# A two-layer expert trunk on one core: gate matrix by one matmul per token, v rows by fours

## Chip, core and metric

One core of one Trainium2 chip. The metric is the device time of one execution in microseconds (us); three runs of the kernel before gave 3102.27 to 3110.34, median 3108.2.

## What is computed

Two layers over 512 tokens of width 1024, in float32. Layer 0 mixes tokens by sliding-window attention, layer 1 by a gated convolution of width 3. After each mixer comes an expert layer that takes most of the work:

```python
def peer_ffn(xn, w_query, sub_keys, expert_u, expert_v):
    q = (xt @ w_query).reshape(T, PEER_HEADS, 2, QUERY_HALF)
    s = jnp.einsum('thpd,hpnd->thpn', q, sub_keys)
    s_top, i_top = lax.top_k(s, PEER_TOPK)
    ...
```

Each of 8 heads chooses 16 of 16384 experts per token, so a token has 128 experts, with a gate for each. Expert e is a row of u and a row of v: the output of a token is the sum over its experts of gate x gelu(x . u[e]) x v[e].

## The kernel before

Tokens are four tiles of 128. The expert layer is done in two ways at once.

Tiles 0 and 1 go the way of `gather` (line 625). For every one of 128 choices an indirect DMA, issued by POOL, fetches the u rows of 128 tokens into a gather tile (line 636), and DVE dots them with x into a column of `act` (line 639). Then for each token an indirect DMA fetches its 128 v rows (line 667), and PE multiplies them by a one-hot column of weights `wd` into 32 rows of `acc` (line 677), four matmuls for a pair of tokens; a manual dependency makes the first of them wait for both rows. Gather tiles come from `gtile` (line 617): GAT = 6 of them, and at times a few more from a pool that another stage leaves free.

Tiles 2 and 3 go the way of `dense` (line 693): all 16384 experts in 128 blocks per layer. `ustep` loads a block of u (`du`), ACT rounds it (`uh`, line 701), DVE takes the rest (`ul`, line 702), PE makes 24 matmuls of 256 columns into `psA` (lines 180 to 183), ACT applies gelu into `dw` (line 712). `vstep` multiplies `dw` by a row of the gate matrix G (line 718; on DVE, or on POOL while a u gather runs), splits it (`wh`, `wl`) and v (`vh`, `vl`), and PE makes 12 matmuls into `y` (line 736).

G holds for each block, token and expert the gate, mostly zero. It is made in chunks of IC = 32 blocks, four chunks per layer, by `gen` (line 739) for TG = 16 tokens at a time. DVE builds a one-hot of the expert's low index (`oj`, line 745), one of its high index (`oi`, line 748), and two products of that with the high and low halves of the gate (line 751). PE multiplies `oj` by each half into the same 32 columns of a PSUM bank, `psG`, one token after the other (line 756), so a group has 32 matmuls. ACT scales the bank into four G buffers of 8 blocks (line 759). `psG` has one bank. G has GB = 5 such buffers of 8 blocks, one of which holds the first gelu results of the layer (`pre`).

The first chunk of a layer is made ahead of its first `vstep`; the next chunks during the last 8 steps (`q0` = 24) of the chunk before. Here "tail" is the end of such a stretch, before the first step that needs the new chunk.

The order of work: `dense`, `gather` and the routing and mixing of the layers are generators that `merge` (line 816) interleaves, by the pace that each yields (`GY` after a group in the first chunk, `rate()` in the gathers). Tile's scheduler then sets the order on every engine from a timeline of its own, with priorities raised by HPG for `gens` and HPV or HPF for the v matmuls. Each engine takes its instructions strictly in that order.

Of the kernel before, what the change touches and what calls it, by code (L numbers as in the profile page):

```python
# [8 lines left out]
F32 = mybir.dt.float32  # L9
# [25 lines left out]
TG = 16  # L35
IC = 32
HC = 8
GAT = 6
# [8 lines left out]
GB = 5  # L47
# [3 lines left out]
GY = 1.7  # L51
# [4 lines left out]
PRE = 1  # L56
# [28 lines left out]
def trunk(ctx: ExitStack, tc: tile.TileContext, a: dict, out: bass.AP):  # L85
# [539 lines left out]
    def gather(l, t, r):  # L625
# [28 lines left out]
        for gr in range(2):  # L654
            acc = pv.tile([P, 512], F32, name="acc", tag="acc")
            for q in range(4):
                wd = gp.tile([P, 2, 8, 32], F32, name="wd", tag="wd", bufs=2)
                wdf = wd.rearrange("p j r c -> p j (r c)")
                nc.gpsimd.memset(wd, 0.0)
                nc.vector.tensor_copy(wdf[:, :, 8 * q:8 * q + 7 * 33 + 1:33],  # L660
                                      wT.rearrange("p (j r) -> p j r", j=4)[:, 2 * gr:2 * gr + 2, 8 * q:8 * q + 8])
                for r8 in range(8):
                    vgs = []
                    for j in range(2):
                        tt = 64 * gr + 32 * j + 8 * q + r8
                        vg = gtile("vg")
                        ld = nc.gpsimd.indirect_dma_start(  # L667
                            out=vg, out_offset=None, in_=a[f"v{l}"],
                            in_offset=bass.IndirectOffsetOnAxis(ap=idxT[:, tt:tt + 1], axis=0))
                        vgs.append(vg)  # L670
                        if j == 0:
                            yield rate()
                    with tc.high_priority(offset=HPF if st.get("front") else HPV):
                        for j in range(2):
                            for h in range(2):
                                c = 32 * (2 * j + h)
                                mm = nc.tensor.matmul(acc[c:c + 32, :], wd[:, j, r8, :],  # L677
                                                      vgs[j][:, h * 512:(h + 1) * 512],
                                                      start=(q == 0 and r8 == 0), stop=(q == 3 and r8 == 7))
                                if j == 0:  # L680
                                    tc.add_manual_dep(mm.ins, ld.ins.name, together, reason="both rows of a pair")
                    yield rate()
# [10 lines left out]
    def dense(l, rs, pool):  # L693
# [11 lines left out]
        def ustep(i):  # L705
# [4 lines left out]
            w = (pre[:, i, :] if i < npre else  # L710
# [4 lines left out]
        def vstep(i):  # L715
            first, last = i == 0, i == NK - 1
            w = ws.pop(i)
            (nc.gpsimd if (WPU if st.get("gu") else WPV) else nc.vector).tensor_tensor(w, w, G[i // HC][:, i % HC, :], op=ALU.mult)
            f = VU if st.get("gu") else VG if i % IC >= 2 * IC - GB * HC else VB0
# [19 lines left out]
        def gen(i, tg):  # L739
# [13 lines left out]
            ps = pmm("psG")  # L753
            for T in range(TG):
                for q in range(2):
                    nc.tensor.matmul(ps[:, T * IC:(T + 1) * IC], oj[:, :, T], oi[:, q, :, T],  # L756
                                     start=(q == 0), stop=(q == 1))
            for hf in range(IC // HC):
                nc.scalar.mul(G[i // HC + hf][:, :, tg * TG:(tg + 1) * TG],  # L759
                              ps.rearrange("p (t i) -> p i t", i=IC)[:, hf * HC:(hf + 1) * HC, :], 1.0 / GSC)  # L760

        NG = T2 // TG
        G = {}

        def gens(c, tg):
            if tg == 0:
                for hf in range(IC // HC):
                    G[c * (IC // HC) + hf] = pool.tile([P, HC, T2], F32, name="G", tag="G", bufs=GB)
            with tc.high_priority(offset=HPG):
                gen(c * IC, tg)  # L770

        npre = HC * PRE
        pre = pool.tile([P, HC, T2], F32, name="pre", tag="G", bufs=GB) if PRE else None
# [6 lines left out]
        for i in range(NK):  # L780
            c, q = divmod(i, IC)
            q0 = 2 * IC - GB * HC
# [211 lines left out]
```

## Time and profile before

| | before |
|---|---|
| median of three runs | 3108.2 us (3102.27 to 3110.34) |
| the profiled execution's own time | 3084.04 us |
| its span in the profile | 3082.2 us |
| PE busy, mean granted clock | 2782.4 us (90%), 0.95 |
| DVE busy | 2255.1 us (73%) |
| ACT, POOL busy | 1178.1 (38%), 1352.1 (44%) |
| DMA | 931.40 MB, mean 302 GB/s |

Busy time of PE is that of its matmuls; weight loads (PEld) stand apart and overlap them. In a row of a group, "idle before" is idle time of that engine right before the group's instructions, and the arrow names what ended it. The granted clock of PE is a share of its full 2.4 GHz, 0.50 being its lower level of 1.2 GHz. Dense steps are numbered 0 to 127 in layer 0 and 128 to 255 in layer 1; the first `y` of layer 0 is at 665 us, that of layer 1 at 2118.

### The profile page before, as it was taken

The numbers are of one execution on the slowest core, as the hardware profiler recorded it, in microseconds if no ns is written. First come the engines' busy times: TensorE is split into PE (matmuls) and PEld (weight loads), VectorE is DVE, ScalarE is ACT, GpSimd is POOL, SyncE is SP. The second block draws the span as 40 slices with busy tenths as digits, with TensorE's granted clock in tenths as the row PEclk, the third lists the DMA queues.
The fourth block names the chain that finished last, engine by engine and source line by source line (L and its number), as shares of the span: only waits on it lengthen the run. The fifth ranks groups of instructions, "written<-read, shape, count | busy, mean of one in ns | idle before, by whom it ended". The sixth has DMA issues, their size and how long they took to land.

```text
span 3082.2 us, 53493 instructions
## 1 busy us (share of the span) xinstructions
PE 2782.4 (90%) x19980; PEld 2242.6 (73%) x19980; DVE 2255.1 (73%) x5363; ACT 1178.1 (38%) x2414; POOL 1352.1 (44%) x1154
## 2 busy tenths in 40 slices
PE   5964799999998999999997798999998798999998
PEld 5862367757986887778776787775787687778776
DVE  2499859887996997455459998887479999456444
ACT  4225433424333334344343334333434333334433
POOL 0157643354354444531347752345326866531331
PEclk8986899979999999999999899997999999999999
DMA  5888888879889977985999996787959988975996
GB/s 193 299 312 307 323 303 292 307 278 359 299 329 381 356 268 260 328 301 178 350 335 387 373 359 220 264 306 270 319 193 377 357 297 321 340 274 182 341 338 215
DMA packets 263205, 931.40 MB, mean 302 GB/s; under 512 B 29984, under 2 KB 38560, under 8 KB 262944
## 3 DMA queue, kind: packets, MB, share of 16 engines
q0 software_dynamic: 147456, 536.94, 48.1%
q1 hardware_dynamic: 115488, 391.03, 35.2%
q8 instruction: 158, 2.59, 0.3%
q14 instruction: 103, 0.84, 0.1%
HBM read 916.31 MB, written 11.53 MB: 301 GB/s over the span
## 4 chain that ended last, share of the span: by engine, by line
PE 72%; DVE 14%; DMA 5%; issue 4%; ACT 3%; POOL 1%; SPq 0%; DVEq 0%; ACTq 0%; POOLq 0%
PE y L736 20%; PE acc L677 9%; PE psG L756 9%; PE psA L180 8%; PE psA L181 7%; PE psA L183 7%; DVE ug L639 7%; PE psrq L568 3%; DMA ug<-in_u_dram,idx 2%; PE psbcu L404 1%; DMA vg<-in_v_dram,idxT 1%; PE psq L241 1%; DVE vl L702 1%; PE psrs L574 1%; PE psrq L180 1%
## 5 line engine op out<-in xcount | busy, mean ns | idle before, releaser
L667 POOL DMA_INDIRECT vg<-in_v_dram,idxT x512 | 550.0, 1074 | 945.7 <-PE acc L677 839.0
L636 POOL DMA_INDIRECT ug<-in_u_dram,idx x512 | 670.3, 1309 | 626.5 <-DVE act L639 269.8
L639 DVE CUSTOM_DVE_ANT_0 ug<-ug,xn 128x1024 f32<-128x1024 f32 x512 | 628.8, 1240 | 27.5 <-DMA ug<-in_u_dram,idx 26.7
L180 PE MATMUL psA<-xh,uh 128*128 128x256 f32 x2048 | 525.5, 294 | 44.7 <-ACT uh L701 26.8
L702 DVE TENSOR_TENSOR ul<-du,uh 128x1024 fp32r<-128x1024 f32 x256 | 316.4, 1236 | 264.5 <-ACT uh L701 244.9
L181 PE MATMUL psA<-xl,uh 128*128 128x256 f32 x2048 | 503.7, 284 | 0.0
L180 PEld LDWEIGHTS psA<-xh,uh 128*128 128x128 f32 x2048 | 391.9, 191 | 147.6 <-ACT wh L724 54.5
L702 DVE TENSOR_TENSOR vl<-dv,vh 128x1024 fp32r<-128x1024 f32 x256 | 319.9, 1249 | 183.5 <-ACT vh L701 169.4
L701 ACT CAST uh<-du 128x1024 fp32r<-128x1024 f32 x256 | 269.5, 1053 | 340.7 <-PE psA L181 296.4
L181 PEld LDWEIGHTS psA<-xl,uh 128*128 128x128 f32 x2048 | 391.5, 191 | 5.3 <-issue 3.0
L701 ACT CAST vh<-dv 128x1024 fp32r<-128x1024 f32 x256 | 268.8, 1051 | 240.8 <-PE y L736 198.3
L677 PE MATMUL acc<-vg,wd 128*32 128x512 f32 x2048 | 315.8, 637 | 10.4 <-DMA vg<-in_v_dram,idxT 10.0
L756 PEld LDWEIGHTS <-oj 128*128 128x128 f16 x4096 | 278.1, 159 | 63.1 <-issue 37.6
L736 PE MATMUL y<-vh,wh 128*128 128x512 f32 x1024 | 291.5, 404 | 26.6 <-ACT vh L701 26.6
L756 PE MATMUL psG<-oi,oj 128*128 128x32 f16 x4096 | 298.4, 249 | 7.6 <-ACT G L759 6.6
L183 PE MATMUL psA<-xh,ul 128*128 128x256 f32 x2048 | 292.2, 284 | 5.3 <-DVE ul L702 5.3
L736 PE MATMUL y<-vl,wh 128*128 128x512 f32 x1024 | 281.7, 397 | 11.6 <-DVE vl L702 11.6
L183 PEld LDWEIGHTS psA<-xh,ul 128*128 128x128 f32 x2048 | 264.4, 190 | 23.5 <-issue 9.2
L736 PE MATMUL y<-vh,wl 128*128 128x512 f32 x1024 | 278.7, 394 | 0.0
L759 ACT ACTIVATE G<-psG 128x128 f32<-128x128 f32 x512 | 102.5, 282 | 366.5 <-PE psG L756 346.2
L745 DVE TENSOR_TENSOR oj<-ijT,iorep 128x2048 f16<-128x2048 f16 x128 | 157.8, 1233 | 108.9 <-PE psG L756 108.6
L736 PEld LDWEIGHTS y<-vh,wh 128*128 128x128 f32 x1024 | 181.1, 192 | 71.4 <-ACT vh L701 35.1
(207 smaller groups left out, 3902.6 us busy)
## 6 DMA issues: line engine op xcount, KB each, us to landing
du<-in_uT_dram SPq DMA_DIRECT2D x256, 512.0 KB, 6.2
dv<-in_v_dram SPq DMA_DIRECT2D x256, 512.0 KB, 6.2
wpc<-in_wq_dram SPq DMA_DIRECT2D x64, 512.0 KB, 5.7
wpc<-in_w_in_dram SPq DMA_DIRECT2D x48, 512.0 KB, 6.7
wpo<-in_wo_dram SPq DMA_DIRECT2D x16, 512.0 KB, 4.5
ug<-in_u_dram,idx POOLq DMA_INDIRECT x512, 7.3
vg<-in_v_dram,idxT POOLq DMA_INDIRECT x512, 6.9
wpo<-in_w_out_dram SPq DMA_DIRECT2D x16, 512.0 KB, 7.3
```

Source lines behind the costliest of these rows:

```text
L180: nc.tensor.matmul(ps, w[0][:, k, :], x[0][:, k, ts], start=(k == 0), stop=False)
L181: nc.tensor.matmul(ps, w[0][:, k, :], x[1][:, k, ts], start=False, stop=False)
L183: nc.tensor.matmul(ps, w[1][:, k, :], x[0][:, k, ts], start=False, stop=(k == KC - 1))
L636: nc.gpsimd.indirect_dma_start(out=ug, out_offset=None, in_=a[f"u{l}"], in_offset=bass.IndirectOffsetOnAxis(ap=r["idx"][h][:, c:c + 1], ax ...
L639: nc.vector.tensor_tensor_reduce(out=ug, in0=ug, in1=xn, scale=1.0, scalar=0.0, op0=ALU.mult, op1=ALU.add, accum_out=act[:, s:s + 1])
L667: ld = nc.gpsimd.indirect_dma_start(out=vg, out_offset=None, in_=a[f"v{l}"], in_offset=bass.IndirectOffsetOnAxis(ap=idxT[:, tt:tt + 1], ax ...
L677: mm = nc.tensor.matmul(acc[c:c + 32, :], wd[:, j, r8, :], vgs[j][:, h * 512:(h + 1) * 512], start=(q == 0 and r8 == 0), stop=(q == 3 and ...
L701: nc.scalar.copy(hi, w)
L702: nc.vector.tensor_tensor(lo, w, hi, op=ALU.subtract)
L736: nc.tensor.matmul(ys[tt][h], x[:, tt * P:(tt + 1) * P], m[:, h * 512:(h + 1) * 512], start=first and k == 0, stop=last and k == len(terms ...
L745: nc.vector.tensor_tensor(oj, jT.unsqueeze(1).to_broadcast([P, P, TG]), iorep, op=ALU.is_equal)
L756: nc.tensor.matmul(ps[:, T * IC:(T + 1) * IC], oj[:, :, T], oi[:, q, :, T], start=(q == 0), stop=(q == 1))
```

## The change

Four things are changed. `gen` takes 8 tokens instead of 16, with one-hot tiles of half the size. Each token has one matmul of 64 columns instead of two of 32 that accumulate: the products with the high and the low half of the gate stand in separate columns of the bank, and the addition moves to the evacuation, where ACT writes the first half scaled into G and DVE adds the second with scalar_tensor_tensor. G is one ring of GR = 40 rows instead of five buffers of 8; where a chunk's 32 rows pass the end of the ring the evacuation is in two pieces. And `gather` multiplies four v rows at a time, when all four have come, from GAT = 8 gather tiles. In the new kernel the `psG` matmul is line 758, ACT's piece 767, DVE's addition 768, `oj` 747, `oi` 750 and 753, the u dots 638, `ul` and `vl` 704, `uh` and `vh` 703, gelu 714, the multiplication by G 720, `wl` 727.

```diff
-TG = 16
+TG = 8
 IC = 32
-HC = 8
-GAT = 6
+TP = 8
+GAT = 8
...
-GB = 5
+GR = 40
...
-GY = 1.7
+GY = 0.85
...
-PRE = 1
@@ -659,26 +658,29 @@
                 nc.gpsimd.memset(wd, 0.0)
                 nc.vector.tensor_copy(wdf[:, :, 8 * q:8 * q + 7 * 33 + 1:33],
                                       wT.rearrange("p (j r) -> p j r", j=4)[:, 2 * gr:2 * gr + 2, 8 * q:8 * q + 8])
-                for r8 in range(8):
-                    vgs = []
-                    for j in range(2):
-                        tt = 64 * gr + 32 * j + 8 * q + r8
+                for r8 in range(0, 8, 2):
+                    vgs, lds = [], []
+                    for n in range(4):
+                        tt = 64 * gr + 32 * (n % 2) + 8 * q + r8 + n // 2
                         vg = gtile("vg")
                         ld = nc.gpsimd.indirect_dma_start(
                             out=vg, out_offset=None, in_=a[f"v{l}"],
                             in_offset=bass.IndirectOffsetOnAxis(ap=idxT[:, tt:tt + 1], axis=0))
                         vgs.append(vg)
-                        if j == 0:
+                        lds.append(ld)
+                        if n < 3:
                             yield rate()
                     with tc.high_priority(offset=HPF if st.get("front") else HPV):
-                        for j in range(2):
+                        for n in range(4):
+                            j, r = n % 2, r8 + n // 2
                             for h in range(2):
                                 c = 32 * (2 * j + h)
-                                mm = nc.tensor.matmul(acc[c:c + 32, :], wd[:, j, r8, :],
-                                                      vgs[j][:, h * 512:(h + 1) * 512],
-                                                      start=(q == 0 and r8 == 0), stop=(q == 3 and r8 == 7))
-                                if j == 0:
-                                    tc.add_manual_dep(mm.ins, ld.ins.name, together, reason="both rows of a pair")
+                                mm = nc.tensor.matmul(acc[c:c + 32, :], wd[:, j, r, :],
+                                                      vgs[n][:, h * 512:(h + 1) * 512],
+                                                      start=(q == 0 and r == 0), stop=(q == 3 and r == 7))
+                                if n < 3:
+                                    for ld in lds[n + 1:]:
+                                        tc.add_manual_dep(mm.ins, ld.ins.name, together, reason="rows of four")
                     yield rate()
             for j in range(2):
                 for h in range(2):
@@ -707,7 +709,7 @@
             u = pool.tile([P, KC, P], F32, name="du", tag="raw", bufs=RB)
             nc.sync.dma_start(u, a[f"uT{l}"][i])
             mm3(ps[:, :T2], halves(u, [P, KC, P], "u"), (xh, xl), slice(0, T2))
-            w = (pre[:, i, :] if i < npre else
+            w = (G[:, IC + i, :] if i < npre else
                  pool.tile([P, T2], F32, name="dw", tag="dw", bufs=LAG + 2))
             nc.scalar.activation(w, ps[:, :T2], AF.Gelu)
             ws[i] = w
@@ -715,8 +717,8 @@
         def vstep(i):
             first, last = i == 0, i == NK - 1
             w = ws.pop(i)
-            (nc.gpsimd if (WPU if st.get("gu") else WPV) else nc.vector).tensor_tensor(w, w, G[i // HC][:, i % HC, :], op=ALU.mult)
-            f = VU if st.get("gu") else VG if i % IC >= 2 * IC - GB * HC else VB0
+            (nc.gpsimd if (WPU if st.get("gu") else WPV) else nc.vector).tensor_tensor(w, w, G[:, i % GR, :], op=ALU.mult)
+            f = VU if st.get("gu") else VG if i % IC >= 2 * IC - GR else VB0
             sp = int((i + 1) * f) > int(i * f)
             if sp:
                 wh = pool.tile([P, T2], F32R, name="wh", tag="wh", bufs=2)
@@ -750,27 +752,30 @@
             for q in range(2):
                 nc.vector.tensor_tensor(oi[:, q], oi[:, 2],
                                         rr["gb"][:, q:q + 1, t0:t0 + TG].to_broadcast(sh), op=ALU.mult)
-            ps = pmm("psG")
-            for T in range(TG):
-                for q in range(2):
-                    nc.tensor.matmul(ps[:, T * IC:(T + 1) * IC], oj[:, :, T], oi[:, q, :, T],
-                                     start=(q == 0), stop=(q == 1))
-            for hf in range(IC // HC):
-                nc.scalar.mul(G[i // HC + hf][:, :, tg * TG:(tg + 1) * TG],
-                              ps.rearrange("p (t i) -> p i t", i=IC)[:, hf * HC:(hf + 1) * HC, :], 1.0 / GSC)
+            for part in range(TG // TP):
+                ps = pmm("psG")
+                for T in range(TP):
+                    nc.tensor.matmul(ps[:, T * 2 * IC:(T + 1) * 2 * IC].rearrange("p (q i) -> p q i", q=2),
+                                     oj[:, :, part * TP + T], oi[:, 0:2, :, part * TP + T], start=True, stop=True)
+                psv = ps.rearrange("p (t q i) -> p q i t", q=2, i=IC)
+                tok = slice(tg * TG + part * TP, tg * TG + (part + 1) * TP)
+                r0 = i % GR
+                cut = min(IC, GR - r0)
+                for o, n, row in ((0, cut, r0), (cut, IC - cut, 0)):
+                    if n:
+                        g = G[:, row:row + n, tok]
+                        nc.scalar.mul(g, psv[:, 0, o:o + n, :], 1.0 / GSC)
+                        nc.vector.scalar_tensor_tensor(g, psv[:, 1, o:o + n, :], 1.0 / GSC, g,
+                                                       op0=ALU.mult, op1=ALU.add)
 
         NG = T2 // TG
-        G = {}
+        G = pool.tile([P, GR, T2], F32, name="G")
 
         def gens(c, tg):
-            if tg == 0:
-                for hf in range(IC // HC):
-                    G[c * (IC // HC) + hf] = pool.tile([P, HC, T2], F32, name="G", tag="G", bufs=GB)
             with tc.high_priority(offset=HPG):
                 gen(c * IC, tg)
 
-        npre = HC * PRE
-        pre = pool.tile([P, HC, T2], F32, name="pre", tag="G", bufs=GB) if PRE else None
+        npre = GR - IC
         for i in range(LAG + npre):
             ustep(i)
             yield 1.0
@@ -779,7 +784,7 @@
             yield GY
         for i in range(NK):
             c, q = divmod(i, IC)
-            q0 = 2 * IC - GB * HC
+            q0 = 2 * IC - GR
             if q >= q0 and c + 1 < NK // IC:
                 for tg in range((q - q0) * NG // (IC - q0), (q - q0 + 1) * NG // (IC - q0)):
                     gens(c + 1, tg)
```

Groups of `psG` matmuls go from 128 of 32 to 256 of 8, and their evacuation from 512 pieces on ACT to 448 on ACT and 448 on DVE. In PE's order, groups that follow the group before with no other matmul between go from 5 to 85: 12, 2, 10 and 13 by chunk in layer 0, and 13, 6, 11 and 18 in layer 1. Separate stretches of `acc` matmuls go from 238 to 159. Three places show it.

ACT in the tail of layer 0's last chunk, before (`G` is the evacuation, `uh`, `vh`, `dw`, `wh` belong to dense steps):

```order
L759 ACTIVATE G<-psG 128x8x16 x4
L701 CAST uh<-du 128x1024
L712 ACTIVATE dw<-psA 128x256
L759 ACTIVATE G<-psG 128x8x16 x4
L701 CAST vh<-dv 128x1024
L724 CAST wh<-dw 128x256
```

and now:

```order
L767 ACTIVATE G<-psG 128x24x8
L703 CAST uh<-du 128x1024
L767 ACTIVATE G<-psG 128x8x8
L714 ACTIVATE dw<-psA 128x256
L703 CAST vh<-dv 128x1024
L714 ACTIVATE dw<-psA 128x256
L767 ACTIVATE G<-psG 128x24x8
L767 ACTIVATE G<-psG 128x8x8
L767 ACTIVATE G<-psG 128x24x8
```

Four pieces in a row, with a dense step's work between, have become pieces of 8 and 24 rows that each have something of their own to wait for; the last rows stand one after the other with nothing between.

DVE at the same place, before (`oj`, `oi` the one-hots, `ul`, `vl`, `wl` the splits of dense steps):

```order
L718 TENSOR_TENSOR dw<-dw,G 128x256
L745 TENSOR_TENSOR oj<-ijT,iorep 128x2048
L748 TENSOR_TENSOR oi<-ijT,iorep 128x512
L751 TENSOR_TENSOR oi<-oi,gb 128x512 x2
L702 TENSOR_TENSOR vl<-dv,vh 128x1024
L725 TENSOR_TENSOR wl<-dw,wh 128x256
L745 TENSOR_TENSOR oj<-ijT,iorep 128x2048
```

and now:

```order
L753 TENSOR_TENSOR oi<-oi,gb 128x256 x2
L704 TENSOR_TENSOR ul<-du,uh 128x1024
L768 SCALAR_TENSOR_TENSOR G<-psG,G 128x8x8
L704 TENSOR_TENSOR vl<-dv,vh 128x1024
L747 TENSOR_TENSOR oj<-ijT,iorep 128x1024
L750 TENSOR_TENSOR oi<-ijT,iorep 128x256
L768 SCALAR_TENSOR_TENSOR G<-psG,G 128x24x8
L753 TENSOR_TENSOR oi<-oi,gb 128x256 x2
L768 SCALAR_TENSOR_TENSOR G<-psG,G 128x8x8
L747 TENSOR_TENSOR oj<-ijT,iorep 128x1024
```

One group's one-hots now stand around the two additions of the group before: `oj` and `oi` ahead of the first, the two gated `oi` between them.

DVE beside dense steps and a u gather in layer 1, one step, before (`ug`, `act` are a dot and its sum):

```order
L702 TENSOR_TENSOR vl<-dv,vh 128x1024
L725 TENSOR_TENSOR wl<-dw,wh 128x256
L639 ISA ug,act<-ug,xn 128x1024
L639 ISA act 128x1
L702 TENSOR_TENSOR ul<-du,uh 128x1024
L718 TENSOR_TENSOR dw<-dw,G 128x256
L639 ISA ug,act<-ug,xn 128x1024
L639 ISA act 128x1
L639 ISA ug,act<-ug,xn 128x1024
L639 ISA act 128x1
```

and now:

```order
L704 TENSOR_TENSOR ul<-du,uh 128x1024
L727 TENSOR_TENSOR wl<-dw,wh 128x256
L638 ISA ug,act<-ug,xn 128x1024
L638 ISA act 128x1
L638 ISA ug,act<-ug,xn 128x1024
L638 ISA act 128x1
L720 TENSOR_TENSOR dw<-dw,G 128x256
L638 ISA ug,act<-ug,xn 128x1024
L638 ISA act 128x1
L638 ISA ug,act<-ug,xn 128x1024
L638 ISA act 128x1
L704 TENSOR_TENSOR vl<-dv,vh 128x1024
```

Three u rows stand beside each dense step before, four now. By dense step 56 of layer 0, DVE has dotted 256 u rows before and 312 now; in layer 1 the second u phase ends at step 192 before and 160 now.

## Rows read from the trace of the kernel before

**Rows 1.** The page: span, busy time by engine, the chain that ended last.
```profile
span 3082.2 us, 53493 instructions
...
PE 2782.4 (90%) x19980; PEld 2242.6 (73%) x19980; DVE 2255.1 (73%) x5363; ACT 1178.1 (38%) x2414; POOL 1352.1 (44%) x1154
...
PE 72%; DVE 14%; DMA 5%; issue 4%; ACT 3%; POOL 1%; SPq 0%; DVEq 0%; ACTq 0%; POOLq 0%
```

**Rows 2.** Busy time by stage: PE, PEld, DVE, ACT, POOL, granted clock, DMA share, GB/s.
```profile
1173.00:1690.00 517.00, 501.21 (x3526) 393.72 (x3525) 313.59 (x457) 206.79 (x364) 213.74 (x195) 0.99 0.85 309
1690.00:2118.00 428.00, 380.65 (x2737) 316.74 (x2738) 380.77 (x1230) 153.00 (x315) 199.65 (x167) 0.91 0.82 298
...
2310.00:2600.00 290.00, 249.34 (x1783) 217.03 (x1781) 281.79 (x415) 110.78 (x211) 207.77 (x145) 0.98 0.93 343
2600.00:3082.00 482.00, 467.31 (x3251) 362.97 (x3249) 238.35 (x317) 185.47 (x324) 162.60 (x157) 0.99 0.79 281
```

**Rows 3.** Groups by line: busy us, mean ns of one, idle before and its releasers.
```profile
L639 DVE CUSTOM_DVE_ANT_0 ug<-ug,xn 128x1024 f32<-128x1024 f32 x512 | 628.8, 1240 | 27.5 <-DMA ug<-in_u_dram,idx 26.7
L667 POOL DMA_INDIRECT vg<-in_v_dram,idxT x512 | 550.0, 1074 | 945.7 <-PE acc L677 839.0 <-issue 78.7 <-PE psi L514 6.5
...
L677 PE MATMUL acc<-vg,wd 128*32 128x512 f32 x2048 | 315.8, 637 | 10.4 <-DMA vg<-in_v_dram,idxT 10.0 <-issue 0.4
L756 PE MATMUL psG<-oi,oj 128*128 128x32 f16 x4096 | 298.4, 249 | 7.6 <-ACT G L759 6.6 <-DVE oi L751 0.3
...
L745 DVE TENSOR_TENSOR oj<-ijT,iorep 128x2048 f16<-128x2048 f16 x128 | 157.8, 1233 | 108.9 <-PE psG L756 108.6
...
L759 ACT ACTIVATE G<-psG 128x128 f32<-128x128 f32 x512 | 102.5, 282 | 366.5 <-PE psG L756 346.2 <-POOL dw L718 15.8 <-DVE pre L718 1.7
L751 DVE TENSOR_TENSOR oi<-oi,gb 128x512 f16<-128x512 f16 x256 | 98.2, 425 | 1.2
...
L712 ACT ACTIVATE dw<-psA 128x256 f32<-128x256 f32 x240 | 91.8, 383 | 164.9 <-PE psA L183 164.6
```

**Rows 4.** Timeline at full clock, 1402.5 to 1407: start, duration, engine, operation.
```profile
1402.98 1.06 PE L677 MATMUL acc<-vg,wd 128*32 128x512 f32 x8
...
1403.98 2.28 PE L756 MATMUL psG<-oi,oj 128*128 128x32 f16 x32
...
1406.07 0.36 PE L180 MATMUL psA<-xh,uh 128*128 128x256 f32 x1
...
1406.27 0.28 PE L181 MATMUL psA<-xl,uh 128*128 128x256 f32 x1
...
1406.29 0.79 ACT L759 ACTIVATE G<-psG 128x128 f32<-128x128 f32 x4 [2.76 <-PE psG L756]
...
1406.39 0.28 PE L180 MATMUL psA<-xh,uh 128*128 128x256 f32 x1
```

**Rows 5.** Timeline in the first chunk's tail of layer 0, 636 to 642.
```profile
636.05 1.93 PE L677 MATMUL acc<-vg,wd 128*32 128x512 f32 x6
...
637.91 2.34 PE L756 MATMUL psG<-oi,oj 128*128 128x32 f16 x32
...
640.17 2.79 PE L677 MATMUL acc<-vg,wd 128*32 128x512 f32 x12
...
641.43 0.42 DVE L748 TENSOR_TENSOR oi<-ijT,iorep 128x512 f16<-128x512 f16 x1
641.76 0.42 DVE L751 TENSOR_TENSOR oi<-oi,gb 128x512 f16<-128x512 f16 x1
```

**Rows 6.** Timeline, 403 to 406.
```profile
403.35 1.92 PE L677 MATMUL acc<-vg,wd 128*32 128x512 f32 x16
```

**Rows 7.** DVE groups by form, those that read PSUM.
```profile
L210 DVE TENSOR_TENSOR x<-x,pswo 128x512 f32<-128x512 f32 x12 | 8.2, 686 | 34.9 <-PE pswo L206 29.4 <-PE pswo L204 5.5
...
L409 DVE TENSOR_TENSOR cc<-psbcu,cc 128x128 f32<-128x128 f32 x8 | 2.3, 287 | 3.9 <-PE psbcu L404 3.9
```

**Rows 8.** PE's granted clock in that tail, columns as in rows 2.
```profile
635.00:640.00 5.00, 5.00 (x54) 3.25 (x53) 3.31 (x15) 0.79 (x4) 1.46 (x2) 0.50 0.04 6
```

## The prediction

> **What bounds the kernel now.** The page comes first: TensorE (PE) is busy 90% of the span and holds 72% of the chain that ended last, VectorE (DVE) 73% and 14% [rows 1]. Averages hide stages, so busy time by stage is next [rows 2]. Where dense steps run without a u gather, PE is busy 97% (501.21 of 517, 467.31 of 482): there a microsecond taken from PE is one off the span. From 1690 to 2118 PE and DVE each have 381 of 428, and from 2310 to 2600 DVE has 281.79 of 290 against PE's 249.34: u rows are dotted beside dense steps there and DVE sets the pace. The groups by line give the prices [rows 3]: the gate matmuls `psG` are 4096, `acc` 2048, the u dots 512 x 1240 ns on DVE.
>
> The profiled execution took 3084.04, 24.2 under the median of the three runs, 3108.2. The sum below is a difference against that execution, and I add it to the median. About 0.3%, 9 us, is what a measurement of this kernel can tell from no change.
>
> **The change, part by part (us).**
>
> A. Fewer gate matmuls on PE. A group of 32 starts at 1403.98 and the next matmul at 1406.07 [rows 4]: 2.09, or 65 ns each. At half clock a group takes 2.34 to its last end [rows 5]; by starts (637.91 to 640.17 for the next matmul) 2.26, or 71 ns. 64 columns at full clock occupy the array as long as 32 at half clock, so I take 71: 8 x 0.071 = 0.57. Before: 128 x 2.09 = 268. After: 256 x 0.57 = 145, and 128 more switches of weights at about 0.08 each, 10. **-113**. Bounds: -124 at 65 ns, and -16 at the 0.12 us between starts of 256-column matmuls (1406.27 to 1406.39). The Trainium skill, "TensorE: Matmul & The Clock Gate", section "Back-to-back issue gap", states 81 ns for sustained 128-column matmuls with their loads; an estimate by that figure, 2048 x 0.081 = 166, makes the saving 92. No run here shows it, and the trace's 65 ns at 32 columns neither supports nor excludes it.
>
> B. Quads. A run of 8 `acc` matmuls takes 1.06 [rows 4], one of 16 takes 1.92 [rows 6]: joining two saves 0.20. The order has 238 separate stretches of `acc` before and 159 now: 79 x 0.20 = **-16** (0 to -32).
>
> C. The gate bank's chain, a new wait. `psG` has one PSUM bank. Until now four ACT pieces empty it in 0.79 while PE does other work; the whole wait of `psG` on ACT is 6.6 [rows 3]. Now each group needs ACT, then DVE, and in chunks 1 to 3 of each layer ACT, DVE, ACT, DVE in turn, before PE may write again. While a u and a v step stand between groups that is covered: 24 matmuls at 0.12 and 12 of twice the columns, about 5.5. It is not where groups stand back to back, 85 of 256 in the order (5 of 128 before): 25 with one piece in the first chunks, 60 with two in the tails of the others. Prices: ACT takes 282 for 128 elements and 383 for 256 [rows 3], so 0.23 for 64. DVE from PSUM takes 287 for 128 and 686 for 512 [rows 7], so 0.22 for 64, 0.35 for 192, 0.42 for 256. Two-piece period: matmuls 0.78 with the 0.22 in which the last one drains, ACT 0.23, 0.05 for the hop, DVE 0.22, then the two gated `oi` that the order puts between DVE's pieces, 0.51 (ACT's second piece runs beside them), DVE 0.35, hop 0.05: 2.2. One piece: 0.78 + 0.38 + 0.05 + 0.42 + 0.05 = 1.7. Less the 0.64 already in A: 60 x 1.56 + 25 x 1.06 = **+121**. Bounds: a period of 1.4, were the `oi` done ahead and the hops free, +65; 3.2, were every second hop behind another 1.2 us operation such as `ul` or `uh`, +213. The Trainium skill, "PSUM — Partial Sum Buffer", section "PSUM bank collisions raise a hardware error", says that two engines may not touch one bank's partitions at once, even to read. Without that rule ACT's second piece could run beside DVE's first, an estimate of 0.3 less per two-piece period, 18 in all; no run here shows it, since only ACT reads this bank so far.
>
> D. After a tail. While groups run back to back, the multiplications by G of the steps behind them collect on DVE, some nine of 0.42; the first y waits for one, the rest must be caught up: about 3 in each of six tails, **+18** (0 to 23).
>
> E. PE's clock. In the first chunk's tail before, PE runs at a granted 0.50 [rows 8], the lower of its two levels, after a stretch of short bursts with gaps, and acc stretches take 1.93 where full clock gives 1.06 for more [rows 4, 5]. Bursts of 0.6 every 2.2 invite the same in six more places. Half of the first 5 us after each is 2.5: **+15** (0 to 30).
>
> F. More DVE work. One-hots: 1.23 + 3 x 0.43 per 16 tokens [rows 3], 2.19 by starts, since each starts about 0.09 before the last one's end (641.43, 641.76 [rows 5]). Half the size is not half the time: slope 0.52 ns per element and 0.16 fixed, from 2048 and 512 elements, give 1.27 per 8 tokens, so +0.35 x 128 = 45. The additions from PSUM: 64 of 0.42 and 384 pairwise 0.22 + 0.35, less 0.09 of overlap each: 101. Together 146 of occupancy. It lies on the path only where DVE is the limit, the stages with u gathers: about 100 of 256 groups, 57, and DVE is at 89 to 97% there, not 100 [rows 2]. **+45** (0 to 146).
>
> G. Eight gather tiles for six. POOL's v loads wait 839.0 for `acc` to free a tile and DVE's dots wait 26.7 for u rows [rows 3]. PE's own wait for v rows is 10.0. The waits on POOL cost nothing where PE is behind; I take **-10** (0 to -27). A quad holds its tiles longer, which eats part of two more.
>
> H. Gathers come earlier: four u rows beside each dense step against three, layer 1's second u phase done by dense step 160 of the numbering in which layer 1 starts at 128, against 192. The same rows are dotted, so 0 (-40 to +60: DVE is fuller for fewer steps, and PE fuller later). ACT's gate pieces go from 512 x 282 ns to 448 of 0.23 to 0.38 and ACT is at 38%: 0. The G ring frees rows one by one instead of by eight; `du` and `dv` loads keep their four tiles: 0.
>
> Sum: -113 - 16 + 121 + 18 + 15 + 45 - 10 = **+60: 3168**.
>
> **The rivals.**
>
> 1. Faster. The chain stays short (1.4, +65), tails leave no backlog and no low clock, and DVE's extra work hides except from 2310 to 2600, about 32 groups x 0.57 = 18: -113 - 16 + 65 + 18 - 10 = -56, **3052**. For it: the saving is on the engine that bounds, and PE at 97% over a thousand microseconds takes it in full. Against it: the order shows 85 groups back to back, and a stall there is PE's own. It decides where C to F together come below 139, roughly a two-piece period under 2.2 with DVE's work hidden.
>
> 2. Slower still. Every second hop waits behind a 1.2 us operation, 60 x 2.56 + 25 x 1.56 = 193, and DVE's extra is worth 75: -113 - 16 + 193 + 18 + 15 + 75 - 10 = +162, **3270**. For it: DVE's and ACT's queues are in order, and `ul`, `vl`, `uh`, `vh` stand between the pieces at the start of each tail. Against it: deeper in a tail the order has nothing but one-hots and pieces.
>
> 3. No change: the cancellation lands within 9 us, **3108**. No mechanism holds it there; it is a strip between 1 and the forecast.
>
> 4. The change does not do what it says: 64 columns take the 256-column pace, PE saves 16 instead of 113, +157, **3265**. Against it: at half clock 32 columns take 71 ns.
>
> **How the numbers follow.** Forecast 0.5 (its own range 3118 to 3230), rival 1 0.27, rival 2 0.11, no change 0.08, rival 4 0.04. The order is certain, the durations come from neighbouring rows, but C and F hang on where queues stand, so the range reaches from just below rival 1 to just short of rival 2: 3045 to 3255, leaving out the ends of both, some 2 in 10. Faster by over 0.3%: 0.28; within: 0.09; slower: 0.63.
>
> **What would show it.** A: a stretch of eight `psG` starts 0.57 before the next matmul. C: `psG` idle before, released by DVE's addition, near 120 in total, and ACT's pieces waiting for DVE; if that idle time is under 60, C failed and rival 1 holds. D, E: DVE's G multiplications in a row after each tail; granted clock 0.5 to 0.8 in the last stretch before dense steps 32, 64, 96. F: additions of 0.22 to 0.42, DVE at 90% and more in the u-gather stages and PE's share lower there. B: `acc` in stretches of 16 of 1.9. Wrong altogether if the stages without u gathers, 1173 to 1690 and 2600 to 3082, shrink by more than PE saves, or if the gathers' new place lengthens the end of layer 1.

## The result, and the profile after

The changed kernel takes 3419.6 us (median of four runs, 3417.23 to 3422.31) where the kernel before takes 3105.2 beside it: 1.1013 times as long, 95% interval 1.099 to 1.1035, 314 us slower. The forecast was 60 slower and its range ended at 3255.

The page of the changed kernel, answering to [rows 1]:

```profile
span 3417.4 us, 50203 instructions
...
PE 2815.2 (82%) x17932; PEld 2253.2 (66%) x17932; DVE 2391.6 (70%) x6323; ACT 1203.5 (35%) x2350; POOL 1337.7 (39%) x1154
```

PE's busy time has not fallen, 2815.2 against 2782.4, though 2048 gate matmuls are gone; its share has, 82% against 90%. The mean granted clock fell from 0.95 to 0.899. The groups, answering to [rows 3]:

```profile
L678 PE MATMUL acc<-vg,wd 128*32 128x512 f32 x2048 | 315.9, 670 | 23.3 <-DMA vg<-in_v_dram,idxT 23.0
...
L758 PE MATMUL psG<-oi,oj 128*128 128x64 f16 x2048 | 297.0, 303 | 240.9 <-DVE G L768 233.0 <-issue 2.1 <-DVE oi L753 1.8
...
L747 DVE TENSOR_TENSOR oj<-ijT,iorep 128x1024 f16<-128x1024 f16 x256 | 178.7, 699 | 247.1 <-PE psG L758 198.2 <-issue 25.6 <-remote 14.2
L768 DVE SCALAR_TENSOR_TENSOR G<-psG,G 128x64 f32<-128x64 f32 (+3 forms) x448 | 137.2, 306 | 23.9 <-ACT G L767 23.4 <-issue 0.4
L767 ACT ACTIVATE G<-psG 128x64 f32<-128x64 f32 (+3 forms) x448 | 130.6, 292 | 579.0 <-PE psG L758 346.2 <-DVE G L768 141.8 <-issue 49.3
...
L753 DVE TENSOR_TENSOR oi<-oi,gb 128x256 f16<-128x256 f16 x512 | 128.1, 293 | 0.2
```

`psG` was idle before for 7.6 and is now for 240.9, of which 233.0 was ended by DVE's addition; the waits of PE say in how many cases, and the longest:

```profile
PE psG L758 <- DVE G L768: 233.0, 96, 7.8
```

2048 matmuls of 64 columns are busy as long, 297.0, as 4096 of 32 were, 298.4. Counted from start to start (up to 0.55 after each matmul as work, the rest as a wait) PE's time on `psG` went from 279 to 295, the wait for it from 12 to 224, the wait for `y` from 33 to 71, for `acc` from 15 to 38; all of PE's work from 2796 to 2844, all of its waits from 265 to 553. That is, but for rounding, the 335 between the two spans (the profiled execution of before ran 21 under its median, so the medians differ by 314). By stretch, from the starts of the first matmuls of each:

| stretch | before | after |
|---|---|---|
| start to the first `psA` of layer 0 | 535 | 566 |
| first `psA` to first `y`, layer 0 / layer 1 | 131 / 127 | 201 / 190 |
| dense steps 0 to 31, layer 0 / layer 1 | 258 / 236 | 339 / 329 |
| dense steps 32 to 63 | 319 / 271 | 319 / 289 |
| dense steps 64 to 95 | 250 / 252 | 295 / 250 |
| dense steps 96 to the last `y` | 190 / 193 | 158 / 157 |

The first chunks and the dense steps 0 to 31 lose most; the last stretch, which generates nothing and now has its gathers behind it, wins back 32 and 36. The stretches do not hold the same work before and after. In layer 0, 85 of PE's time in steps 0 to 31 goes to matmuls of mixing and routing, where it was 32, and none in steps 32 to 63, where it was 59; so steps 32 to 63 lose about as much as they shed. In layer 1, steps 0 to 31 have 115 u dots beside them, where they had 25, and steps 32 to 63 none, where they had 103. Busy time by stage, columns as in [rows 2], for the first chunk of layer 0, a stretch without gate groups in chains, one with two tails, the first chunk of layer 1, the stretch to its first tail, and the end:

```profile
566.00:768.00 202.00, 134.50 (x945) 101.31 (x946) 183.95 (x666) 54.83 (x109) 116.34 (x100) 0.78 0.90 333
...
1107.00:1291.00 184.00, 181.81 (x1177) 135.05 (x1176) 86.59 (x139) 71.51 (x118) 96.08 (x95) 0.99 0.89 320
1291.00:1905.00 614.00, 485.18 (x2989) 411.47 (x2988) 439.50 (x810) 222.97 (x399) 212.67 (x169) 0.88 0.69 245
...
2191.00:2380.00 189.00, 129.57 (x902) 87.03 (x901) 151.97 (x615) 53.16 (x105) 93.69 (x89) 0.78 0.82 294
2380.00:2709.00 329.00, 255.11 (x1434) 194.70 (x1435) 276.37 (x553) 97.56 (x185) 216.93 (x159) 0.87 0.92 346
...
2997.00:3417.00 420.00, 373.31 (x2343) 332.53 (x2340) 236.86 (x409) 174.54 (x300) 30.02 (x24) 0.91 0.44 147
```

PE is at 99% and full clock from 1107 to 1291, and at 67% and a granted 0.78 in the first chunk of layer 0, where DVE has 183.95 of 202.

Two stretches of the timeline show what one group costs. Groups back to back with nothing else (tail of layer 1's last chunk), start, duration, engine:

```profile
3206.86 1.17 PE L758 MATMUL psG<-oi,oj 128*128 128x64 f16 x8 [1.79 <-DVE G L768]
3208.07 0.33 ACT L767 ACTIVATE G<-psG 128x192 f32<-128x192 f32 x1 [1.54 <-PE psG L758]
3208.07 0.69 DVE L747 TENSOR_TENSOR oj<-ijT,iorep 128x1024 f16<-128x1024 f16 x1 [1.26 <-PE psG L758]
3208.68 0.28 DVE L750 TENSOR_TENSOR oi<-ijT,iorep 128x256 f16<-128x256 f16 x1
3208.88 0.35 DVE L768 SCALAR_TENSOR_TENSOR G<-psG,G 128x192 f32<-128x192 f32 x1
3209.14 0.48 DVE L753 TENSOR_TENSOR oi<-oi,gb 128x256 f16<-128x256 f16 x2
3209.26 0.22 ACT L767 ACTIVATE G<-psG 128x64 f32<-128x64 f32 x1 [0.86 <-DVE G L768]
3209.54 0.22 DVE L768 SCALAR_TENSOR_TENSOR G<-psG,G 128x64 f32<-128x64 f32 x1
3209.82 0.91 PEld L758 LDWEIGHTS <-oj 128*128 128x128 f16 x8 [2.06 <-DVE G L768]
3209.82 1.17 PE L758 MATMUL psG<-oi,oj 128*128 128x64 f16 x8 [1.79 <-DVE G L768]
```

From 3206.86 to 3209.82 is 2.96. PE's eight matmuls end 1.2 after the start. DVE then does `oj` and `oi`, 0.8, ahead of the first addition, since `oj` waits for the same end of PE; the first addition, the gated `oi`, the second addition follow one by one, and ACT's second piece waits for DVE's first. Now a tail beside a u gather, layer 0:

```profile
1405.48 1.22 DVE L638 CUSTOM_DVE_ANT_0 ug<-ug,xn 128x1024 f32<-128x1024 f32 x1
...
1405.63 1.17 PE L758 MATMUL psG<-oi,oj 128*128 128x64 f16 x8 [5.02 <-DVE G L768]
...
1406.62 1.22 DVE L638 CUSTOM_DVE_ANT_0 ug<-ug,xn 128x1024 f32<-128x1024 f32 x1
1406.83 0.28 ACT L767 ACTIVATE G<-psG 128x128 f32<-128x128 f32 x1 [3.85 <-PE psG L758]
...
1407.77 0.69 DVE L747 TENSOR_TENSOR oj<-ijT,iorep 128x1024 f16<-128x1024 f16 x1
...
1408.38 0.29 DVE L750 TENSOR_TENSOR oi<-ijT,iorep 128x256 f16<-128x256 f16 x1
1408.58 0.29 DVE L768 SCALAR_TENSOR_TENSOR G<-psG,G 128x128 f32<-128x128 f32 x1
1408.78 1.22 DVE L638 CUSTOM_DVE_ANT_0 ug<-ug,xn 128x1024 f32<-128x1024 f32 x1
1408.90 0.28 ACT L767 ACTIVATE G<-psG 128x128 f32<-128x128 f32 x1 [1.79 <-DVE G L768]
...
1409.92 1.23 DVE L638 CUSTOM_DVE_ANT_0 ug<-ug,xn 128x1024 f32<-128x1024 f32 x1
...
1411.06 0.49 DVE L753 TENSOR_TENSOR oi<-oi,gb 128x256 f16<-128x256 f16 x2
...
1411.47 0.29 DVE L768 SCALAR_TENSOR_TENSOR G<-psG,G 128x128 f32<-128x128 f32 x1
...
1411.82 1.17 PE L758 MATMUL psG<-oi,oj 128*128 128x64 f16 x8 [5.02 <-DVE G L768]
```

From 1405.63 to 1411.82 is 6.19. Four u dots of 1.22 stand on DVE in it: two ahead of the one-hots, beside PE's matmuls and ACT's first piece, and two between the two additions. From the last start of one back-to-back group to the first of the next it is most often 2.08 to 2.12, the bare chain, and 5.31 in three cases in which four dots begin; the gate part alone (e3) has 3.23 with two dots, 4.38 with three, 5.31 with four and 6.46 with five. Of the 240.9 that PE idles before `psG`, 27 waits with a dot in them make 94 and 76 without one make 147.

### The profile page after: what moved, and what is told of

It is laid out like the page before. It is cut to its first block, busy times and chain, and to the rows that moved or that the text cites. A ratio compares the mean times of both kernels' runs of the same rounds, so it can differ in the third digit from the quotient of the medians.

```text
span 3417.4 us, 50203 instructions
## 1 busy us (share of the span) xinstructions
PE 2815.2 (82%) x17932; PEld 2253.2 (66%) x17932; DVE 2391.6 (70%) x6323; ACT 1203.5 (35%) x2350; POOL 1337.7 (39%) x1154
## 5 line engine op out<-in xcount | busy, mean ns | idle before, releaser
L635 POOL DMA_INDIRECT ug<-in_u_dram,idx x512 | 677.6, 1323 | 520.5 <-DVE act L638 153.4
L179 PE MATMUL psA<-xh,uh 128*128 128x256 f32 x2048 | 518.3, 291 | 44.0 <-ACT uh L703 22.2
L758 PE MATMUL psG<-oi,oj 128*128 128x64 f16 x2048 | 297.0, 303 | 240.9 <-DVE G L768 233.0
L758 PEld LDWEIGHTS <-oj 128*128 128x128 f16 x2048 | 234.4, 148 | 329.3 <-DVE G L768 168.5
L747 DVE TENSOR_TENSOR oj<-ijT,iorep 128x1024 f16<-128x1024 f16 x256 | 178.7, 699 | 247.1 <-PE psG L758 198.2
L767 ACT ACTIVATE G<-psG 128x64 f32<-128x64 f32 (+3 forms) x448 | 130.6, 292 | 579.0 <-PE psG L758 346.2
L738 PE MATMUL y<-vh,wh 128*128 128x512 f32 x1024 | 298.4, 415 | 42.4 <-ACT vh L703 26.8
L738 PE MATMUL y<-vh,wl 128*128 128x512 f32 x1024 | 292.1, 408 | 26.9 <-DVE wl L727 26.9
L720 POOL TENSOR_TENSOR dw<-dw,G 128x256 f32<-128x256 f32 x94 | 97.0, 1040 | 466.6 <-ACT dw L714 342.1
```

The costliest lines, as they stand in the source:

```text
L179: nc.tensor.matmul(ps, w[0][:, k, :], x[0][:, k, ts], start=(k == 0), stop=False)
L635: nc.gpsimd.indirect_dma_start(out=ug, out_offset=None, in_=a[f"u{l}"], in_offset=bass.IndirectOffsetOnAxis(ap=r["idx"][h][:, c:c + 1], ax ...
L738: nc.tensor.matmul(ys[tt][h], x[:, tt * P:(tt + 1) * P], m[:, h * 512:(h + 1) * 512], start=first and k == 0, stop=last and k == len(terms ...
L747: nc.vector.tensor_tensor(oj, jT.unsqueeze(1).to_broadcast([P, P, TG]), iorep, op=ALU.is_equal)
L758: nc.tensor.matmul(ps[:, T * 2 * IC:(T + 1) * 2 * IC].rearrange("p (q i) -> p q i", q=2), oj[:, :, part * TP + T], oi[:, 0:2, :, part * TP ...
```

## The experiments

All of them were timed beside the kernel before on the same chip, so ratios are the measure, and microseconds set against the 314 are a difference of ratios times 3105; before took 3110 beside e1 to e4, 3088 beside e5 to e8, 3086 beside e9 and e10, 3106 beside e11 and e12.

**e1, columns from neighbouring values.**

```diff
-oj[:, :, part * TP + T], oi[:, 0:2, :, part * TP + T], start=True, stop=True)
+oj[:, :, part * TP + T], oif[:, (part * TP + T) * 64:(part * TP + T + 1) * 64]
```

> The changed kernel, but each 64-column gate matmul reads 64 neighbouring values of the one-hot product instead of 64 values that lie 16 bytes apart (the gates then belong to the wrong tokens: this kernel leaves the right sorting of the gates out). In the changed kernel's trace gate matmuls start 123 ns apart, as 256-column ones do. Theory (spacing of the moving operand's values sets that): the distance falls to 60 to 75 ns, 2048 x 0.055 = 110 less on PE, part of it inside the back-to-back periods, which fall from 2.97 to about 2.5: 3270 to 3320 us. Rival (64 columns cost this much in any layout, or the weights do): the distance stays at 118 to 126 ns and the time at 3420.

Measured: 3359.9, ratio 1.0824 (1.0796 to 1.0851), 59 less than the change. The median distance between starts is 62 ns against 123. Its group and two of its back-to-back groups:

```profile
L759 PE MATMUL psG<-oi,oj 128*128 128x64 f16 x2048 | 175.0, 236 | 258.2 <-DVE G L769 246.4 <-DVE oi L753 5.7 <-issue 2.9
```

```profile
3149.79 0.70 PE L759 MATMUL psG<-oi,oj 128*128 128x64 f16 x8 [1.79 <-DVE G L769]
3152.28 0.71 PE L759 MATMUL psG<-oi,oj 128*128 128x64 f16 x8 [1.79 <-DVE G L769]
```

The period is 2.49 where it was 2.96; the wait itself is the same 1.79. So the spacing of the columns doubled the price of a 64-column matmul. But only 59 of some 105 that PE's work on `psG` fell by (295 to 190 by starts) came off the time; all of PE's waits grew by 35. Whether the 62 that are left are the columns or the weights, still 16 bytes apart, was not tested.

**e2, weights from neighbouring values.**

```diff
-oj[:, :, part * TP + T], oi[:, 0:2
+ojf[:, (part * TP + T) * P:(part * TP + T + 1) * P], oi[:, 0:2
```

> The changed kernel, but each gate matmul loads its 128 weight columns from 128 neighbouring values of the one-hot tile instead of values 16 bytes apart (the gates come out wrong). Theory (the moving operand's spacing sets the pace): no change, 123 ns and 3420 within 15 us. Rival (the weight load with spaced values sets it): the distance between starts falls to 60 to 80 ns and the time by 80 to 150 us.

Measured: 3422.1, ratio 1.0999 (1.0972 to 1.1026), 116 ns between starts. The theory holds for the time; the distance fell by 7 ns, 18 us of PE's work by starts, which did not come off the time. While columns are spaced, the spacing of the weights matters little.

**e3, the gate part alone** (the diff's part on `gather` undone, GAT = 6).

> The changed kernel with the v rows multiplied in pairs from six gather tiles, as before: the gate part of the change alone. Theory (the gate part makes nearly all of the 314): 3390 to 3450 us, psG idle before still over 180. Rival (fours and the earlier gathers cost a good part, because the gathers crowd the dense steps): 3300 or less.

Measured: 3347.8, ratio 1.0781 (1.0753 to 1.0808). Neither: the gate part makes 242 of the 314, and 72 belong to the gathers, whose sign I had the other way. The first y of layer 0 comes at 697, against 768 in the changed kernel and 665 before.

**e4, halves added in PSUM again.**

```diff
-nc.tensor.matmul(ps[:, T * 2 * IC:(T + 1) * 2 * IC].rearrange("p (q i) -> p q i", q=2), ...
+for q in range(2):
+    nc.tensor.matmul(ps[:, T * IC:(T + 1) * IC], oj[:, :, part * TP + T], oi[:, q, :, part * TP + T], start=(q == 0), stop=(q == 1))
...
-nc.vector.scalar_tensor_tensor(g, psv[:, 1, o:o + n, :], 1.0 / GSC, g, op0=ALU.mult, op1=ALU.add)
```

> The changed kernel, but the two halves of a gate are added in the PSUM bank again, two matmuls of 32 columns per token, and ACT alone empties the bank, in one or two pieces; groups of 8 tokens, the ring and the fours stay. Theory (the addition on DVE, in PE's chain, makes most of the loss): the wait of psG on DVE vanishes, gate matmuls start 65 ns apart, and the time is 3110 to 3180, the rest being the smaller one-hots. Rival (small groups and doubled one-hots make the loss, through DVE's fixed costs and the order): 3250 or more.

Measured: 3265.5, ratio 1.0498 (1.0473 to 1.0524). The addition with its wide matmuls is worth 160 here, but 155 remain. The theory's signs came (no wait on DVE's addition, starts 62 ns apart) and the rival's time (3250 or more): about half is the addition's, half is not. Its `psG` group:

```profile
L759 PE MATMUL psG<-oi,oj 128*128 128x32 f16 x4096 | 308.9, 242 | 95.9 <-DVE oi L753 65.5 <-ACT G L767 12.3 <-issue 5.7
```

The wait on DVE's addition is gone; in its place PE waits 65.5 for `oi`, the one-hots of small groups.

**e5, small groups alone** (e4 with pairs and GAT = 6).

> As the run with the halves added in PSUM (3265), but v rows in pairs from six gather tiles: against the kernel before only the groups and one-hots of 8 tokens, the ring and the pieces of the evacuation are new. Theory (the costs add: fours and eight tiles cost about 72, as 3420 less 3348 says, small groups about 85): 3180 to 3210. Rival (fours cost only where DVE's additions stand in the chain): 3245 or more, and then small groups alone make 140.

Measured: 3155.5, ratio 1.0218 (1.0201 to 1.0235): 68 above its before, and a little under the theory's range, which was set beside a slower before. The rival is out. Small groups, with the ring and its pieces, cost 68, the addition on DVE 0.0563 of before or 175 (e3 less e5), the gathers 72. The costs add only roughly: without the addition the gathers make 0.0280 or 87 (e4 less e5). The `psG` group, idle for 7.6 before:

```profile
L756 PE MATMUL psG<-oi,oj 128*128 128x32 f16 x4096 | 308.1, 241 | 52.9 <-DVE oi L750 41.7 <-ACT G L764 10.0 <-ACT i L454 0.6
```

**e6, fours alone, six tiles.** The diff's hunk on `gather` in the kernel before.

> The kernel before with v rows multiplied in fours, still from six gather tiles, since eight don't fit beside the one-hots of 16 tokens. Theory (fours and the order that follows them cost by themselves): 3150 to 3190. Rival (what costs is u gathers started earlier by eight tiles into a chain with DVE additions): 3095 to 3125, by my term B perhaps 16 less than before.

Measured: 3194.9, ratio 1.0354 (1.0337 to 1.0372), 107 slower. It is on the theory's side and above its range, but the reason may be its own: with six tiles a four leaves two for the next loads.

```profile
L667 POOL DMA_INDIRECT vg<-in_v_dram,idxT x512 | 548.2, 1071 | 1130.3 <-PE acc L679 1014.2 <-issue 74.2 <-PE psA L183 10.7
...
L679 PE MATMUL acc<-vg,wd 128*32 128x512 f32 x2048 | 389.0, 664 | 30.3 <-DMA vg<-in_v_dram,idxT 30.0
```

POOL's v loads wait 1014.2 for `acc`, against 839.0 [rows 3], and the last v row is multiplied at 3181, after the last `y` at 3169. It says what fours cost with six tiles, not what they cost in the change.

**e7, one-hots of 16 tokens in the gate part** (e3 with TG = 16, TP = 8, GY = 1.7).

> The gate part alone (pairs, six tiles, 3348), but one-hots for 16 tokens again, each used by two groups of 8 tokens with 64-column matmuls. Theory (the addition on DVE and the serial bank make most of the 240, the smaller one-hots a part, since oj and oi of the next group stand in the chain ahead of the first addition): 3250 to 3310. Rival (the smaller one-hots make most): 3200 or less. A second rival (they make nothing): 3335 to 3360.

Measured: 3351.1, ratio 1.0854 (1.0835 to 1.0872): no gain over e3's 1.0781, rather a loss. The second rival holds: with the addition in the chain, halving the one-hots' fixed costs gives nothing. Its columns lie 32 bytes apart instead of 16, and starts are 127 ns apart.

**e8, the kernel before with neighbouring values.**

```diff
-oj[:, :, T], oi[:, q, :, T],
+ojf[:, T * P:(T + 1) * P], oif[:, q * 512 + T * IC:q * 512 + (T + 1) * IC],
```

> The kernel before, but gate matmuls load weights and read columns from neighbouring values of the one-hot tiles instead of values 32 bytes apart (the gates come out wrong). Starts are 65 ns apart before. Theory (with spaced columns at 1.9 ns each, 32 columns and the weight load are both at about 60, so neither alone can be seen; with neighbouring values both fall): starts 30 to 50 ns apart and 3010 to 3070. Rival (a floor of the matmul itself at 60): 60 to 65 ns and 3090 to 3115.

Measured: 2989.0, ratio 0.9692 (0.9675 to 0.971), 98 less than before. Starts are 25 ns apart, below what the theory had:

```profile
L758 PE MATMUL psG<-oi,oj 128*128 128x32 f16 x4096 | 128.3, 178 | 21.9 <-DVE oi L751 16.6 <-ACT G L761 4.0
```

PE's time on `psG` falls from 279 to 123 by starts. So 156 of the 279 that the 4096 matmuls of the kernel before took came of how their operands lie, not of their columns or their count.

**e9, one-hot tiles in pairs of tokens**, which leaves every gate with its token:

```diff
-oj = pool.tile([P, P, TG], F16, name="oj", tag="oj", bufs=2)
+oj = pool.tile([P, TG // 2, P, 2], F16, name="oj", tag="oj", bufs=2)
+pr = lambda v, n: v.rearrange("p (a b) -> p a b", b=2).unsqueeze(2).to_broadcast([P, TG // 2, n, 2])
...
-oj[:, :, T], oi[:, q, :, T],
+oj[:, T // 2, :, T % 2], oi[:, q, T // 2, :, T % 2],
```

> The kernel before, with its one-hot tiles laid out in pairs of tokens: weights and columns of a gate matmul then lie 4 bytes apart instead of 32, and DVE still writes two neighbouring tokens at a time. With neighbouring values the matmuls started 25 ns apart and 98 us went. Theory (spacing beyond a few bytes is what slows PE's reads): starts under 40 ns apart, DVE's one-hots at 1.2 and 0.43 as before, 2990 to 3030 where before stands at 3090 to 3110. Rival 1 (any spacing slows them): 60 ns, no change. Rival 2 (DVE pays for the layout: oj goes over 2 us, 130 more on DVE): PE's gain is eaten beside u gathers, no more than 40 us won.

Measured: 2994.2, ratio 0.9699 (0.9682 to 0.9716): faster than both kernels.

```profile
L747 DVE TENSOR_TENSOR oj<-ijT,iorep 128x2048 f16<-128x2048 f16 x128 | 158.8, 1241 | 17.3 <-PE psG L755 17.1
L755 PE MATMUL psG<-oi,oj 128*128 128x32 f16 x4096 | 128.4, 178 | 22.7 <-DVE oi L751 17.5 <-ACT G L758 3.8
...
L758 ACT ACTIVATE G<-psG 128x128 f32<-128x128 f32 x512 | 102.4, 283 | 208.5 <-PE psG L755 186.8 <-POOL dw L718 15.1 <-DVE pre L718 3.4
```

Starts are 25 ns apart, `oj` takes 1241 as before (1233), and ACT's pieces 283. Both parts of the theory hold.

**e10, three buffers for one-hots in the gate part** (`oj` and `oi` with bufs=3 in e3).

> The gate part alone (3348 on a chip where before took 3110), with three buffers for each one-hot tile instead of two. In the back-to-back stretches of the changed kernel oj waits until PE has ended the group before, and then oj and oi, 0.8, stand on DVE ahead of the first addition. Theory (that puts 0.4 to 0.5 into each two-piece period): the period falls from 2.97 to about 2.5, 20 to 40 us less. Rival (ACT, the additions and the dots between them set the period, and DVE's order stays): within 10 us.

Measured: 3325.9, ratio 1.0772 (1.0751 to 1.0793), as e3. The period did not move:

```profile
3122.61 1.17 PE L755 MATMUL psG<-oi,oj 128*128 128x64 f16 x8 [1.79 <-DVE G L765]
...
3123.81 0.69 DVE L744 TENSOR_TENSOR oj<-ijT,iorep 128x1024 f16<-128x1024 f16 x1 [1.26 <-PE psG L755]
...
3124.62 0.35 DVE L765 SCALAR_TENSOR_TENSOR G<-psG,G 128x192 f32<-128x192 f32 x1
...
3125.57 1.16 PE L755 MATMUL psG<-oi,oj 128*128 128x64 f16 x8 [1.79 <-DVE G L765]
```

DVE runs one group further ahead, and `oj` still waits for the end of the same PE group. The wait was not taken away, so what it is worth was not measured.

**e11, pairs with eight tiles** (e3 with GAT = 8).

> The gate part with eight gather tiles, but v rows still in pairs: between the gate part alone (pairs, six tiles, 1.0781 of before) and the changed kernel (fours, eight tiles, 1.1013). Theory (what the second part costs comes of gathers that start earlier, which the two more tiles bring: u dots then stand on DVE inside the first chunk's chain): 1.092 to 1.105 of before, and the first y of layer 0 near 760 as in the changed kernel. Rival (the fours cost it: four loads have to be there before a multiplication, and tiles come free four at a time): 1.070 to 1.083, first y near 697.

Measured: 3393.0, ratio 1.0927 (1.0899 to 1.0954), first y of layer 0 at 768, that of the changed kernel. Two more tiles make 0.0146, 45; fours on top make 0.0086, 27.

**e12, e9 with a seventh tile** (GAT = 7).

> The kernel before with one-hot tiles in pairs of tokens (0.9699 of before), and the room that the smaller table of indices leaves taken by a seventh gather tile. Theory (in the kernel before, DVE's dots wait 27 for u rows and PE 10 for v rows, and more tiles save part of that): 0.962 to 0.969. Rival (gathers that start earlier crowd DVE, as in the changed kernel): 0.971 to 0.985.

Measured: 3035.8, ratio 0.9779 (0.9758 to 0.9799). The rival: a seventh tile costs 25. The second u phase of layer 0 runs from 712 to 1050 instead of 709 to 1120, that of layer 1 starts 75 earlier, at 2144 for 2219, and the time is longer.

## Why the prediction was wrong

The sign was right; the size was a fifth of what came. Step by step:

A (-113) failed, and most plainly. Rival 4's condition came true: 64 columns take 123 ns, the pace of 256-column matmuls, and by starts `psG` costs 295, 16 more than before. I had taken from [rows 5] that 64 columns at full clock cost what 32 cost at half clock. But the clock does not set the price of these matmuls: before, the median distance between their starts is 66 ns at full clock and 67 at a granted 0.50, in the changed kernel 123 and 122, while `psA` matmuls of 256 columns go from 117 to 213. What sets it is how the operands lie: 64 columns take 62 with neighbouring columns (e1), and 32 take 25 with neighbouring operands (e8). With values 16 bytes apart 32 columns take 62 (e4) and 64 take 123, so the merge gains nothing. Rival 4 had the pace of this step right, with a chance of 0.04; it had PE save 16, where PE paid 16 more. The Trainium skill's figure in "TensorE: Matmul & The Clock Gate", section "Back-to-back issue gap", 81 ns for 128 columns with their loads, is for a width that no gate matmul has; the 64 spaced columns take more than that all the same, 123. The measurements decide. A rule that I had missed bears on it: the Trainium skill, "SBUF — State Buffer", section "Door 1: The DMA port swizzle (why `[64,N]` ≈ `[32,N]`)", has SBUF in lines of 16 bytes, full speed only for consecutive reads in one line, and a penalty for each that goes to a new one. The runs agree: at 32 columns, 62 to 66 ns where every value lies in a line of its own (e4, before), and 25 ns at 4 bytes (e9).

C (+121) had the mechanism and not the size: `psG` waits 224, 212 more than before. 191 of it stands between 84 groups back to back, where the order had 85: the count was right and the period was not, 3.69 on average where the two worked out make 2.05. The bare two-piece period is 2.96, not 2.2: 0.42 by the matmuls of step A, and some 0.4 because `oj` and `oi` of a coming group stand on DVE ahead of the first addition; I had put only the gated `oi` into the period, though the order showed the other two in front of it. Beside u gathers one to four dots more stand there, which my upper bound of 3.2 did not reach. ACT's second piece waits for DVE's first in every such period, as the Trainium skill, "PSUM — Partial Sum Buffer", section "PSUM bank collisions raise a hardware error", would have it; whether it had to, no run here tells.

F (+45): the occupancy was close, DVE's busy time rose by 136.5 against 146 worked out. That fixed costs of small one-hots lie on the path was wrong in the gate part (e7 gained nothing), while small groups by themselves cost 68 (e5), of which 45 shows as PE's idle time before `psG`, most of it ended by `oi`.

G (-10) and H (0) failed in sign. Two more tiles cost 45 (e11) and fours 27: the dots come earlier, from 692 on, inside a first chunk that now ends at 768, and there they stand on DVE in the chain. The first chunk of layer 0 has no dot and takes 156 in e3, 43 dots and 204 in e11; that of layer 1 has none and takes 163 in e11, 13 and 190 in the changed kernel. That the dots are the cause is read from these traces; no run moved them alone. I had priced the order's move of the dots at nothing because the dots are the same; by these traces their place is what counted. B (-16) had the order right, 238 stretches of `acc` to 159 in the traces, but `acc` falls only from 285 to 281 by starts. That the first `psA` comes 32 later is seen in every run with eight tiles (564 to 572). 64 more `acc` matmuls stand ahead of it, 304 for 240, which with their waits make 11; the cause of the rest was not found.

E (+15) came out near: the granted clock fell to 0.78 in both first chunks, 0.83 and 0.84 before, and to 0.87 to 0.91 in the stages with long tails. It costs nothing in `psG`, whose starts are as far apart at 0.50. In `y` 114 neighbouring starts stand at 0.50, where 24 did, 427 ns apart for 228 at full clock, some 18; in `psA` 105 for 73, some 3. PE's work other than `psG` grew by some 30 by starts in all.

D (+18): the wait for `y` grew by 38.

One path through the runs, e5, e3, e11 and the changed kernel, parts the 314 into 68 for small groups, 175 for additions and wide matmuls, 45 for two tiles and 27 for fours. These are differences of neighbours, so they add up by construction; in another order the shares change, as e4 less e5 shows. No run removed the dots from the chain: the 27 waits that hold one make 94, of which the bare 1.79 each would make 48, so some 45 are theirs, read from the trace alone. No run gave `psG` a second bank either, or the changed kernel operands that both lie close together, so what the chain costs without step A is not shown.

Some sums of the prediction do not come out of their own terms: C makes 120 and not 121, its upper bound 218 and not 213, A's bound at 0.12 us with the 10 for switches, a saving of 12 and not 16, the additions in F 96 and not 101. None of this changes which steps failed.

## What to carry to other kernels

Ask of every matmul whether its columns, its weights or the reading of either sets the distance between starts, before merging two into one: here the layout of the operands was worth 91 (e9) and the merge nothing. A distance that is the same at both levels of the clock is a sign that something else than the columns sets it. When an evacuation passes from one engine to two in turn, write down everything that stands in each queue between the links, one period in full, and count how many groups have no cover. More buffers for a side stream start it earlier; look at what it will stand in front of.

## What the hardware showed that I had not expected

Columns 16 bytes apart cost 1.9 ns each (123 ns for 64), at either level of the clock; with neighbouring columns and weights 16 bytes apart a matmul of 64 took 62, and with 32 columns and both 2 or 4 bytes apart 25. Values 4 bytes apart were read as fast as neighbours, and DVE wrote that layout at its old pace, 1241 against 1233 for 2048 values.
